# Expert stage of a hybrid decoder layer: a written-out order of blocks, a fifth row buffer and paired keys

## The chip, the core and the metric

The kernel runs on one core of a Trainium2 chip. Its engines are TensorE (PE, with its weight loads as PEld), VectorE (DVE), ScalarE (ACT), GpSimd (POOL) and SyncE (SP); SP issues most transfers, POOL issues the ones that fetch rows by index. The metric is the device time of one execution in microseconds. Before the change the median of three executions is 2899.98 us (2895.31 to 2903.27).

## The reference, cut to what matters

One layer over 1024 tokens of width 1024. A mixing part (projection, pooling, a chunked scan, output projection) is followed by retrieval among 16384 single-neuron experts, and a last norm.

```python
q = (hf @ w_query).reshape(T, 8, 2, 128)
s1, s2 = q[:, :, 0] . sub_keys1, q[:, :, 1] . sub_keys2      # 128 scores each
v1, i1 = top_k(s1, 16); v2, i2 = top_k(s2, 16)
cand = v1[..., :, None] + v2[..., None, :]
top_s, pos = top_k(cand, 16); idx = i1 * 128 + i2 at pos
gates = softmax(top_s)                                       # 8 heads x 16 experts a token
u = expert_down[idx]; act = gelu(hb . u); v = expert_up[idx]
y = sum(gates * act * v);  x = x + gate_f * y;  out = rmsnorm(x, norm_final)
```

## The kernel before, in words

The 1024 tokens are eight tiles of 128. The front (`front`, three groups of tiles) does the mixing part, the query projection and, per head, the two lists of 16 best keys (`top16`); `select` turns the lists of one tile into experts and gates.

The experts are reached in two ways. Tiles 1 to 4 (`DT`) are **dense**: `select` builds one-hot matrices (names `hota`, `hotb`, `hotc`, L826 to L843) and from them a table of gates over all 16384 experts in memory (`gd`), and the loop of `experts` then multiplies the 512 tokens with every expert. One turn of it is a **block** of 128 experts: `raw` (512 KB of down weights) is loaded and split into a high part `dnh` (ACT, L1023) and a low part `dnl` (DVE, L1024); the **first product** is 24 matmuls into `m` (L1033); ACT takes GELU (L1036) and DVE multiplies by the gates (L1037), which gives `w`; the **second product** adds `w` times `up` (512 KB) into eight outputs of 128x512 (L1007, two passes each for one block). Four outputs stay in PSUM (`res`), four are made in two rotating buffers (`rot`) and added by DVE to sums `ys` in SBUF (L1012, L1014). Blocks are grouped in units of three (`SB`), and a unit's whole second product stands behind the first product of the next unit's first block.

Tiles 0, 5, 6 and 7 (`GT`) are **gathered**: for each of a tile's 128 expert slots POOL fetches one row of 8 KB for each token (1 MB in all, L907) into one of four row buffers; DVE takes the dot product with the token (L910), ACT the GELU and the gate (L911, L912), and DVE adds the second half of the row to `yacc` (L903); the buffer is then free. Tile 0 goes first in another form (`ahead`): half rows, first all dots and then all adds (L870, L875, L879), as far as possible during the front. `finish` scales, adds the residual, norms and stores a tile. Tiles 6 and 7 have their `top16` and `select` inside the loop.

The order on each engine is made by a scheduler that runs the program on a timeline of its own, takes what is ready by priority, and so mixes the loop with the steps of the gathers, which `drain` emits at a low priority after each block. Each engine runs its list strictly in order. Pools of the expert stage are laid over memory of the front, and each tile waits until what lay there is done. `rows` turns through the row buffers: three of their own and `row3` (in the pool `more`) once `experts` has begun.

Of the kernel before, what the change touches and what calls it, by code (L numbers as in the profile page):

```python
# [44 lines left out]
LEAD = 2  # L45
# [3 lines left out]
MORE = 1  # L49
# [16 lines left out]
class Trunk:  # L66
    def __init__(self, ctx, tc, I, out):
        self.ctx, self.tc, self.nc, self.I, self.out = ctx, tc, tc.nc, I, out
        self.bg = []
        self.due, self.owed, self.few = 0, 0, 2  # L70
        self.early, self.taken = None, 0

# [30 lines left out]


    def consts(self):
# [9 lines left out]
        self.rooms = {name: self.pool(name) for name in ("rz", "rx", "rp", "r1")}  # L115
# [269 lines left out]
    def front(self, gi):  # L385
# [183 lines left out]
        for b in range(16):  # L569
            if gi + 1 < len(GROUPS):  # L570
                if b == 0:
                    xs = self.loads(gi + 1)
                if b == NB:
                    self.scaled(xs)
                    ahead = self.norm1(gi + 1, xs)
                if b >= NB + 2:
                    next(ahead, None)
            wq = self.wload(I["w_q"][b])
            acc = psa.tile([128, 512], FT, name="acc")
            for k in range(KB):  # L580
# [12 lines left out]
            keys = self.kp.tile([128, 128], FT, name="keys")  # L593
            nc.sync.dma_start(keys, I["keysT"][:, b])
            sp = pss.tile([128, 512], FT, name="ss")
            for i in range(n):
                nc.tensor.matmul(sp[:, i * 128:(i + 1) * 128], q[:, i * 128:(i + 1) * 128], keys,
                                 start=True, stop=True)
            self.drain(rate)
            self.fetch(self.frate)  # L600
            sc = self.sp.tile([128, 3, 128], FT, name="sc")
            nc.scalar.activation(sc[:, :n].rearrange("p a b -> p (a b)"), sp[:, :T], AF.Copy)
            for i in range(n):
                if tiles[i] in LATE:
# [3 lines left out]
                scr = self.tp.tile([128, 128], FT, name="tscr", bufs=2)  # L608
                self.top16(sc[:, i], v[:, b // 2, b % 2], pi[:, b // 2, b % 2], scr)
# [98 lines left out]
    def selects(self, lp):  # L708

        for t, v, pi in self.late:  # L710
            for h in range(0, 8, 2):
                sc = lp.tile([128, 4, 128], FT, name="sc")
                self.nc.sync.dma_start(sc, self.scd[LATE.index(t), :, 2 * h:2 * h + 4])
                for b in range(4):
                    scr = self.tp.tile([128, 128], FT, name="tscr", bufs=2)
                    self.top16(sc[:, b], v[:, h + b // 2, b % 2], pi[:, h + b // 2, b % 2], scr)
                    if b % 2:
                        yield
            yield from self.select(t, v, pi)
# [14 lines left out]
    def select(self, t, v, pi):  # L734
# [15 lines left out]
        key = tp.tile([128, 8, 2, 16], BF, name="key")  # L750
        nc.vector.tensor_copy(key, pi)
# [3 lines left out]
        for h in range(8):  # L755
            scr = tp.tile([128, 128], FT, name="tscr", bufs=2)
            self.top16(cand[:, h], top[:, h], pos[:, h], scr[:, :NCAND])
            if h % 2:
                yield
# [12 lines left out]
        for start, length in ROWS:  # L772
            nc.vector.tensor_scalar(q, p, float(start), float(length - (start == SINGLE)), op0=OP.is_ge, op1=OP.mult)
            nc.vector.tensor_tensor(r2, r2, q, op=OP.subtract)
            if start < SINGLE:
                nc.vector.tensor_scalar(q, p, float(start), None, op0=OP.is_ge)
                nc.vector.tensor_tensor(r1, r1, q, op=OP.add)  # L777
        yield
        idx = tp.tile([128, 2, 8, 16], FT, name="idx")
        for j, r in enumerate((r1, r2)):  # L780
            for h in (0, 4):
# [4 lines left out]
                nc.vector.tensor_tensor(oh, oh, key[:, hs, j].unsqueeze(3).to_broadcast([128, 4, 16, 16]), op=OP.mult)  # L786
# [101 lines left out]
    def gather(self, j):  # L888
# [3 lines left out]
        h2 = gp.tile([128, D], FT, name="h2", bufs=1)  # L892
        nc.sync.dma_start(h2, self.h2r[j * 128:(j + 1) * 128, :])
# [11 lines left out]
        for s in range(128):  # L905
# [9 lines left out]
            prev = (u, a, s)  # L915
            yield
        add(*prev)
# [5 lines left out]
        self.finish(t, [acc[:, :512], acc[:, 512:]], rows, self.residual(xx[:, :D], t), xx[:, D:])  # L923
        yield

    def finish(self, t, y, rows, x, tmp, soon=False):
# [3 lines left out]
        for h in range(2):  # L930
# [3 lines left out]
            self.square(tmp[:, hs], x[:, hs], sums[:, 0, h + 1:h + 2])  # L934
        ss = sums[:, 1, 1:2]
        nc.vector.tensor_reduce(ss, sums[:, :1, :3], axis=AX.X, op=OP.add)  # L936
        rs = self.rsqrt(ss, 1)
        for h in range(2):
# [3 lines left out]
            nc.sync.dma_start(self.out[t * 128:(t + 1) * 128, hs], x[:, hs])  # L942

# [10 lines left out]
    def experts(self):  # L954
# [5 lines left out]
        self.more = self.pool("more", reuse_waits="tile")  # L960
        kinds = {"ys": ([128, 512], FT, len(outs) - 4), "up": ([128, D], FT, SB + 4),
                 "gates": ([128, TD // TC, GS, TC], FT, 2), "h2h": ([128, KB, TD], FR, 1), "h2l": ([128, KB, TD], FR, 1),
                 "raw": ([128, D], FT, 3), "dnh": ([128, D], FR, 2), "dnl": ([128, D], FR, 2),
                 "w": ([128, TD], FT, SB + 1)}
# [4 lines left out]

        rot = self.pool("prot", 2, space=PSUM)  # L970
        res = self.pool("pres", 1, space=PSUM)
        pm1 = self.pool("pm1", 2, space=PSUM)
        held = {o: res.tile([128, 512], FT, name=f"res{i}") for i, o in enumerate(outs[:4])}
# [8 lines left out]
        lp = self.pool("late", 2, reuse_waits="tile")  # L982
        self.bg += [self.early, self.mixed(self.gather(EARLY), self.selects(lp), 3)]
        self.bg += [self.gather(j) for j in range(EARLY + 1, len(GT))]
        steps = 129 * len(GT) - self.taken + 40
        gates = None
        done = 0
        queue = []
# [4 lines left out]
        def mm2(u, ws, some=outs):  # L993
            for o in some:
# [13 lines left out]
                if whole:  # L1008
                    sums[o] = ps
                elif o in ysum:  # L1010
                    if u == 0:
                        nc.vector.tensor_copy(ysum[o], ps)  # L1012
                    else:
                        nc.vector.tensor_tensor(ysum[o], ps, ysum[o], op=OP.add)  # L1014

        b = 0
        for u, size in enumerate(units):
            ws = []
            for j in range(size):
                raw = new("raw")  # L1020
                nc.sync.dma_start(raw, I["downT"][b])
                dn = new("dnh"), new("dnl")
                nc.scalar.activation(dn[0], raw, AF.Copy)  # L1023
                nc.vector.tensor_tensor(dn[1], raw, dn[0].bitcast(FT), op=OP.subtract)  # L1024
                if b % GS == 0:
                    gates = new("gates")
                    nc.sync.dma_start(gates, self.gd[b // GS])
                up = new("up")
                nc.sync.dma_start(up, I["ud"][b * 128:(b + 1) * 128, D:])
                p1 = pm1.tile([128, 512], FT, name="m1")  # L1030
                for n, (x, y) in enumerate(((0, 0), (1, 0), (0, 1))):
                    for k in range(KB):
                        nc.tensor.matmul(p1, dn[x][:, k * 128:(k + 1) * 128], h2[y][:, k],  # L1033
                                         start=(k == 0 and n == 0), stop=(k == KB - 1 and n == 2))
                act = new("w")
                nc.scalar.activation(act, p1, AF.Gelu)  # L1036
                nc.vector.tensor_tensor(act.rearrange("p (c t) -> p c t", t=TC),  # L1037
                                        act.rearrange("p (c t) -> p c t", t=TC), gates[:, :, b % GS], op=OP.mult)
                ws.append((act, up))
                if queue and j == (u == last):  # L1040
                    mm2(*queue.pop())
                b += 1
                want = min(steps * b // (NK - SB * LEAD), steps)
                self.drain(want - done)
                done = want
            queue.append((u, ws))
# [3 lines left out]
        sums = dict(held)  # L1050
        for i in reversed(range(nt)):
            mm2(*queue[0], [(i, 0), (i, 1)])
# [88 lines left out]
```

## Time and profile before

| | |
|---|---|
| median of three executions | 2899.98 us |
| profiled execution, whole | 2912.44 us |
| its span, first to last instruction | 2910.6 us |
| TensorE busy | 2663.1 us (91%) |
| VectorE busy | 2375.6 us (82%) |
| bytes moved | 893.31 MB, mean 307 GB/s |

The profiled execution is 2 us longer than its span and 12 us longer than the median. The front takes about the first 1200 us, the dense loop runs from 1221 us, and what follows its last first product, at 2791 us, is a tail of 120 us. A share of busy time is a mean over these stages, so each is read by itself.

### The profile page before, as it was taken

Reading aid. Unit: us, or ns where it says so; the run is one execution under the profiler, and the core shown is the slowest. Engines: PE = TensorE matmul, PEld = TensorE weight load, DVE = VectorE, ACT = ScalarE, POOL = GpSimd, SP = SyncE. Lnnn points to the kernel's source line nnn. Section 1 sums busy time; section 2 is a strip of 40 time slices with the busy share of each in tenths; the row PEclk is TensorE's granted clock in tenths of the full one; section 3 lists DMA queues with packets and bytes.
Section 4 is the critical chain, followed back from the end, with each engine's and each line's share of the span. In section 5 each row is a group of like instructions: output and inputs, shape, how many; then the busy total and the mean of one; then the engine's idle time right before and its main releaser. Section 6 shows DMA issues by size and latency. Waiting matters only on the chain. (4 is left out here: it accounts for less than half of the span.)

```text
span 2910.6 us, 31644 instructions
## 1 busy us (share of the span) xinstructions
PE 2663.1 (91%) x10243; PEld 1746.7 (60%) x10244; DVE 2375.6 (82%) x5156; ACT 830.1 (29%) x2244; POOL 884.6 (30%) x679
## 2 busy tenths in 40 slices
PE   8899986789889989699999999999999999999961
PEld 5688555676557876465655666666666666666630
DVE  6625898979999879899999777787877777778887
ACT  3523451322254342322222222222222222222211
POOL 0000066554440005022333333333333333333343
PEclk9999987899989989899999999999999999999985
DMA  8655389999863679888999999899999989998986
GB/s 304 222 172 173 103 296 331 356 362 361 289 234 124 185 220 383 277 310 323 352 354 356 356 366 337 336 364 361 346 348 351 370 320 372 348 368 339 356 320 234
DMA packets 264278, 893.31 MB, mean 307 GB/s; under 512 B 25904, under 2 KB 110000, under 8 KB 212656
## 3 DMA queue, kind: packets, MB, share of 16 engines
q0 software_dynamic: 92448, 541.11, 49.0%
q1 hardware_dynamic: 171664, 350.18, 34.7%
q8 instruction: 81, 1.33, 0.2%
q14 instruction: 85, 0.70, 0.1%
HBM read 840.86 MB, written 50.34 MB: 306 GB/s over the span
## 5 line engine op out<-in xcount | busy, mean ns | idle before, releaser
L907 POOL DMA_INDIRECT row<-in_ud,eidx x384 | 547.5, 1426 | 1105.8 <-DVE yacc L903 870.4
L903 DVE SCALAR_TENSOR_TENSOR yacc<-row,act,yacc 128x1024 f32<-128x1024 f32 x381 | 488.5, 1282 | 67.9 <-ACT act L912 65.1
L910 DVE SCALAR_TENSOR_TENSOR row<-row,h 128x1024 f32<-128x1024 f32 x384 | 467.1, 1218 | 51.1 <-DMA row<-in_ud,eidx 50.8
L1007 PE MATMUL rot<-up,w 128*128 128x512 f32 x1024 | 464.5, 596 | 4.8 <-DVE ys L1014 4.8
L1007 PE MATMUL res<-up,w 128*128 128x512 f32 x1024 | 458.6, 592 | 0.0
L870 POOL DMA_INDIRECT row<-in_ud,eidx x256 | 313.6, 1225 | 417.3 <-DVE rkb L777 102.1
L911 ACT ACTIVATE act<-act 128x1 f32<-128x1 f32 x384 | 77.1, 201 | 976.0 <-DVE row L910 975.6
L1007 PEld LDWEIGHTS rot<-up,w 128*128 128x128 f32 x1024 | 194.9, 191 | 221.8 <-issue 208.3
L1007 PEld LDWEIGHTS res<-up,w 128*128 128x128 f32 x1024 | 193.8, 189 | 200.5 <-issue 189.4
L1033 PE MATMUL m<-h2h,dnh 128*128 128x512 f32 x1024 | 292.9, 427 | 18.9 <-ACT dnh L1023 18.9
L1033 PE MATMUL m<-h2l,dnh 128*128 128x512 f32 x1024 | 285.6, 413 | 0.0
L1033 PE MATMUL m<-h2h,dnl 128*128 128x512 f32 x1024 | 279.6, 412 | 0.0
L1033 PEld LDWEIGHTS m<-h2h,dnh 128*128 128x128 f32 x1024 | 193.5, 189 | 96.8 <-issue 39.5
L307 PE MATMUL acc<-wraw,r 128*128 128x256 f32 x1024 | 239.3, 388 | 8.3 <-ACT s L525 8.3
L435 PE MATMUL acc<-r,wraw 128*128 128x384 f32 (+1 forms) x768 | 235.0, 464 | 2.3 <-ACT s L439 1.3
L581 PE MATMUL acc<-rz,wraw 128*128 128x384 f32 (+1 forms) x768 | 235.3, 457 | 0.0
L1033 PEld LDWEIGHTS m<-h2l,dnh 128*128 128x128 f32 x1024 | 192.6, 188 | 66.5 <-issue 30.4
L1033 PEld LDWEIGHTS m<-h2h,dnl 128*128 128x128 f32 x1024 | 193.4, 189 | 59.2 <-issue 19.1
L307 PEld LDWEIGHTS acc<-wraw,r 128*128 128x128 f32 x1024 | 196.3, 195 | 37.9 <-ACT s L525 9.9
L1014 DVE TENSOR_TENSOR ys<-rot,ys 128x512 f32<-128x512 f32 x168 | 115.4, 687 | 112.1 <-PE rot L1007 111.6
L435 PEld LDWEIGHTS acc<-r,wraw 128*128 128x128 f32 x768 | 147.7, 195 | 81.8 <-issue 8.6
L581 PEld LDWEIGHTS acc<-rz,wraw 128*128 128x128 f32 x768 | 143.7, 194 | 64.0 <-issue 2.3
(298 smaller groups left out, 3271.3 us busy)
## 6 DMA issues: line engine op xcount, KB each, us to landing
up<-in_ud SPq DMA_DIRECT2D x128, 512.0 KB, 7.4
raw<-in_downT SPq DMA_DIRECT2D x128, 512.0 KB, 7.9
gd<-stage SPq DMA_DIRECT2D x32, 1024.0 KB, 9.3
gates<-gd SPq DMA_DIRECT2D x16, 2048.0 KB, 12.3
wraw<-in_w_c SPq DMA_DIRECT2D x48, 512.0 KB, 5.6
wraw<-in_w_q SPq DMA_DIRECT2D x48, 512.0 KB, 6.3
wraw<-in_w_o SPq DMA_DIRECT2D x36, 512.0 KB, 5.2
row<-in_w_ada SPq DMA_DIRECT2D x32, 512.0 KB, 5.3
```

Of the source, the lines that this page charges most:

```text
L307: self.nc.tensor.matmul(acc[i], a(4 * kp + j, slice(i * 128, (i + 1) * 128)), ws[:, j * 256:(j + 1) * 256], start=kp == kps[0] and j == 0 ...
L435: nc.tensor.matmul(acc[:, :T], wc[:, k * 128:(k + 1) * 128], h[:, k], start=k == 0, stop=k == KB - 1)
L581: nc.tensor.matmul(acc[:, :T], wq[:, k * 128:(k + 1) * 128], g[:, k], start=k == 0, stop=k == KB - 1)
L870: nc.gpsimd.indirect_dma_start(out=u[:, i * D:(i + 1) * D], out_offset=None, in_=src, in_offset=bass.IndirectOffsetOnAxis(ap=e[:, s + i:s ...
L903: nc.vector.scalar_tensor_tensor(acc, u[:, D:], a, acc, op0=OP.mult, op1=OP.add)
L907: nc.gpsimd.indirect_dma_start(out=u, out_offset=None, in_=self.I["ud"], in_offset=bass.IndirectOffsetOnAxis(ap=e[:, s:s + 1], axis=0))
L910: nc.vector.scalar_tensor_tensor(u[:, :D], u[:, :D], 1.0, h2, op0=OP.mult, op1=OP.mult, accum_out=a)
L911: nc.scalar.activation(a, a, AF.Gelu)
L1007: nc.tensor.matmul(ps, w[:, ts], up[:, hs], start=st, stop=sp, skip_group_check=True)
L1014: nc.vector.tensor_tensor(ysum[o], ps, ysum[o], op=OP.add)
L1033: nc.tensor.matmul(p1, dn[x][:, k * 128:(k + 1) * 128], h2[y][:, k], start=(k == 0 and n == 0), stop=(k == KB - 1 and n == 2))
```

## The change

1. Order. From the first block on, every PE, DVE and ACT instruction of the loop is tied to the one before it (`in_order`): the three engines keep the program's order there. SP and POOL are still ordered by the scheduler.
2. The loop is written as a pipeline: raw weights are loaded three blocks ahead, the high part is made two ahead, the low part one ahead, the gates are multiplied one block late, and the second product of a unit is cut in thirds (3, 3 and 2 outputs) behind the first products of the next unit; DVE's additions of `rot` come one block later.
3. Gathers. Tile 0 is drained wholly ahead of the loop. The 384 gather steps of tiles 5, 6, 7 are spread evenly over blocks 4 to 125 (`FIRST`, `LAST`), at most five in a block; one step of `selects` goes to eight of a gather (`MIX`), for the tile that comes next. A gathered tile is finished on DVE, in two steps.
4. A fifth row buffer (`MORE = 2`); the two of the pool `more` are now laid behind the loop's other pools, which themselves stand in another order.
5. `select`: keys are kept twice, side by side, so that the product of one-hot and key reads pairs; a compare and an add become one instruction; one scratch buffer `tscr` for two.

```diff
-LEAD = 2
+FIRST, LAST = 4, 2
+MIX = 8
-MORE = 1
+MORE = 2
...
-        self.rooms = {name: self.pool(name) for name in ("rz", "rx", "rp", "r1")}
+        self.rooms = {name: self.pool(name) for name in ("rx", "rp", "r1", "rz")}
...
-                nc.vector.tensor_scalar(q, p, float(start), None, op0=OP.is_ge)
-                nc.vector.tensor_tensor(r1, r1, q, op=OP.add)
+                nc.vector.scalar_tensor_tensor(r1, p, float(start), r1, op0=OP.is_ge, op1=OP.add)
...
-                nc.vector.tensor_tensor(oh, oh, key[:, hs, j].unsqueeze(3).to_broadcast([128, 4, 16, 16]), op=OP.mult)
+                pairs = oh.rearrange("p h r (a b) -> p (h r) a b", b=2)
+                nc.vector.tensor_tensor(pairs, pairs, key[:, j, hs].rearrange("p h r d -> p (h r) d").unsqueeze(2)
+                                        .to_broadcast([128, 64, 8, 2]), op=OP.mult)
...
-        self.bg += [self.early, self.mixed(self.gather(EARLY), self.selects(lp), 3)]
-        self.bg += [self.gather(j) for j in range(EARLY + 1, len(GT))]
+        self.bg.append(self.early)
+        self.drain()
+
+        start = len(nc.cur_bb.bb.instructions)
+        for j in range(EARLY, len(GT)):
+            late = [s for s in self.late if j + 1 < len(GT) and s[0] == GT[j + 1]]
+            self.bg.append(self.mixed(self.gather(j), self.selects(lp, late), MIX))
+        total = 128 * (len(GT) - EARLY)
...
+                want = total * max(b + 1 - FIRST, 0) // (NK - LAST - FIRST) - self.count
+                want = max(min(want, 5), 0)
+                load(b + 3)
...
+                gated(b - 1)
+                if b % GS == 1:
+                    gload(b // GS + 1)
+                steps(min(want, 1))
+                added()
+                if todo:
+                    n = -(-len(todo) // (size - j))
+                    mm2(u - 1, queue, todo[:n])
+                    todo = todo[n:]
+                    if n > 3:
+                        added()
+                steps(min(max(want - 1, 0), 1))
+                low(b + 1)
+                steps(max(want - 2, 0))
+                acts[b] = new("w")
+                nc.scalar.activation(acts[b], p1, AF.Gelu)
+                high(b + 2)
...
+        gated(NK - 1)
+        added()
+        self.in_order(start)
```

What this does to the order is seen at three places. First POOL, at the end of the front, where `h2h` and `h2l` are the tokens of the dense tiles, `sums` are small cells of the norm, and rows from `in_ud` by `eidx_66` are tile 0's half rows. Before:

```order
L978 DMA h2l<-h2td 128x4096
L870 DMA row_9619<-in_ud,eidx_66 128x1024 x2
L870 DMA row_9707<-in_ud,eidx_66 128x1024 x2
...
L870 DMA row_9912<-in_ud,eidx_66 128x1024 x2
L870 DMA row_9955<-in_ud,eidx_66 128x1024 x2
L933 TENSOR_TENSOR row_9963<-row_9963 128x512 x2
L340 MEMSET sums 128x4 x4
```

And of the change, at the same place:

```order
L1016 DMA h2l<-h2td 128x4096
L353 MEMSET sums 128x4 x3
L892 DMA row_9418<-in_ud,eidx_66 128x1024
L892 DMA row_9423<-in_ud,eidx_66 128x1024 x2
L892 DMA row_9418<-in_ud,eidx_66 128x1024
L892 DMA row_9443<-in_ud,eidx_66 128x1024 x2
...
L892 DMA row_9508<-in_ud,eidx_66 128x1024 x2
L935 DMA row_9749<-in_ud,eidx 128x2048
L935 DMA row_9767<-in_ud,eidx 128x2048
```

The last 32 half rows of tile 0 stood ahead of the cells of `sums`, and stand behind them now (16 rows of two, of which `...` leaves out 13), with tile 5's first gathers right behind.

Second DVE at the same time. Before, tile 0's last additions lie between the one-hots of the front, a hundred rows ahead of the loop's first row:

```order
L879 SCALAR_TENSOR_TENSOR yacc<-row_9912,acts,yacc 128x1024
L828 TENSOR_TENSOR hotc<-hotb,etr 128x1024
L829 TENSOR_TENSOR hotb<-hotb,etr 128x1024
L879 SCALAR_TENSOR_TENSOR yacc<-row_9955,acts,yacc 128x1024 x2
L826 TENSOR_TENSOR hota<-keyno,etr 128x1024
L827 TENSOR_TENSOR hotb<-keyno,etr 128x1024
L932 TENSOR_TENSOR row_9963<-yacc,row_9960 128x512 x2
```

Of the change, in the loop's blocks 2 to 4 (`w` is the product with the gates, L1061 frees a `rot`, `dnl` at the end belongs to block 5):

```order
L1061 COPY ys<-rot 128x512
L1085 TENSOR_TENSOR dnl<-raw,dnh 128x1024
L901 SCALAR_TENSOR_TENSOR yacc<-row_9423,acts,yacc 128x1024
L901 SCALAR_TENSOR_TENSOR yacc<-row_9428,acts,yacc 128x1024 x2
L1090 TENSOR_TENSOR w<-w,gates 128x512
L901 SCALAR_TENSOR_TENSOR yacc<-row_9433,acts,yacc 128x1024 x2
...
L901 SCALAR_TENSOR_TENSOR yacc<-row_9508,acts,yacc 128x1024 x2
L968 TENSOR_TENSOR row_9516<-yacc,row_9513 128x512 x2
L938 SCALAR_TENSOR_TENSOR row_9749,act<-row_9749,h_9746 128x1024
L1061 COPY ys<-rot 128x512
```

38 additions of tile 0 have moved from the front into the loop; 32 of them stand between block 3's product with the gates and the copy that frees a `rot` for block 4, with only tile 0's finish and tile 5's first dot between.

Third DVE where one gathered tile follows another; of the change:

```order
L931 SCALAR_TENSOR_TENSOR yacc<-row_12770,act,yacc 128x1024
L1090 TENSOR_TENSOR w<-w,gates 128x512
L968 TENSOR_TENSOR row_12796<-yacc,row_12793 128x512
L969 TENSOR_TENSOR row_12796<-row_12796 128x512
...
L977 SCALAR_TENSOR_TENSOR row_12796<-row_12796,rs_y,row_12793 128x512 x2
L1063 TENSOR_TENSOR ys<-rot,ys 128x512
L816 SCALAR_TENSOR_TENSOR eidx<-idx 128x128
L938 SCALAR_TENSOR_TENSOR row_12867,act<-row_12867,h_12791 128x1024
L1085 TENSOR_TENSOR dnl<-raw,dnh 128x1024
```

The next tile's indices (`eidx`) are made one instruction ahead of its first dot, and a low part `dnl` stands behind that dot.

## Rows read from the trace of the kernel before

**Rows 1.** the page: span, engines, the queue of gathers, loads to landing
```profile
span 2910.6 us, 31644 instructions
...
q0 software_dynamic: 92448, 541.11, 49.0%
...
up<-in_ud SPq DMA_DIRECT2D x128, 512.0 KB, 7.4
...
gates<-gd SPq DMA_DIRECT2D x16, 2048.0 KB, 12.3
```

**Rows 2.** stretches: length, busy of engines (instructions), PE clock, DMA share, GB/s
```profile
1100.00:1160.00 60.00, 60.00 (x302) 39.17 (x301) 57.89 (x113) 14.64 (x29) 30.17 (x23) 1.00 1.05 392
...
1200.00:1240.00 40.00, 19.63 (x75) 14.42 (x76) 35.57 (x165) 10.61 (x15) 0.28 (x4) 0.70 0.96 344
1300.00:1600.00 300.00, 295.22 (x945) 178.20 (x944) 286.69 (x668) 73.24 (x191) 98.88 (x69) 0.99 0.92 347
1600.00:2000.00 400.00, 400.00 (x1293) 243.48 (x1292) 308.00 (x395) 93.39 (x250) 137.06 (x95) 1.00 0.92 352
...
2804.00:2880.00 76.00, 6.54 (x16) 2.60 (x14) 57.40 (x71) 11.93 (x48) 33.64 (x22) 0.57 0.89 333
```

**Rows 3.** TensorE in order of time, 2795 to 2911: start, length, [idle before]
```profile
2807.80 2.74 PE L1007 MATMUL rot<-up,w 128*128 128x512 f32 x6
2881.54 2.07 PE L1002 MATMUL rot<-ys,ident 128*128 128x512 f32 x2 [71.00 <-DVE dnl L932]
...
2888.24 2.74 PE L1007 MATMUL rot<-up,w 128*128 128x512 f32 x6
```

**Rows 4.** groups of the loop, 1240 to 2790: busy, mean ns | idle before
```profile
L903 DVE SCALAR_TENSOR_TENSOR yacc<-row,act,yacc 128x1024 f32<-128x1024 f32 x352 | 450.6, 1280 | 59.9 <-ACT act L912 57.9 <-DVE yacc L903 0.5
...
L910 DVE SCALAR_TENSOR_TENSOR row<-row,h 128x1024 f32<-128x1024 f32 x356 | 433.1, 1218 | 40.3 <-DMA row<-in_ud,eidx 40.0
...
L1024 DVE TENSOR_TENSOR dnl<-raw,dnh 128x1024 fp32r<-128x1024 f32 x125 | 153.7, 1229 | 10.6 <-ACT dnh L1023 9.2
...
L786 DVE TENSOR_TENSOR oh<-oh,key 128x1024 bf16<-128x1024 bf16 x8 | 9.7, 1218 | 0.1
...
L784 DVE TENSOR_TENSOR oh<-ranks,rkc 128x1024 bf16<-128x1024 bf16 x4 | 2.8, 688 | 0.1
```

**Rows 5.** waits of VectorE, 1600 to 2790: total us, times, longest us
```profile
DVE yacc L903 <- ACT act L912: 55.6, 93, 0.6
...
DVE row L910 <- DMA row<-in_ud,eidx: 27.6, 17, 3.8
```

**Rows 6.** gathers of 1600 to 2790, from issue to landing
```profile
DMA to landing us min/median/max: 2.6/8.5/15.6
```

**Rows 7.** GpSimd in order of time at the front's end
```profile
1150.78 1.26 POOL L870 DMA_INDIRECT row<-in_ud,eidx  x1 [0.30 <-issue]
1205.22 0.17 POOL L340 MEMSET sums<- 128x4 f32 x3 [27.42 <-DVE top L704]
...
1247.03 0.96 POOL L907 DMA_INDIRECT row<-in_ud,eidx  x1 [39.36 <-DVE v L704]
```

**Rows 8.** SyncE at the same time: last gate table stored, first gates loaded
```profile
1205.81 0.62 SPq L848 DMA_DIRECT2D gd<-stage  x1
...
1217.92 0.33 SPq L1027 DMA_DIRECT2D gates<-gd  x1
```

**Rows 9.** tile 0's half rows, issued on GpSimd, 1090 to 1161
```profile
L870 POOL DMA_INDIRECT row<-in_ud,eidx x29 | 38.4, 1324 | 24.4 <-DVE yacc L879 10.7 <-issue 5.5 <-DVE tscr L703 5.3
```

**Rows 10.** tile 0's additions on VectorE, 1100 to 1172
```profile
L879 DVE SCALAR_TENSOR_TENSOR yacc<-row,acts,yacc 128x1024 f32<-128x1024 f32 x30 | 38.2, 1273 | 0.2
```

**Rows 11.** first products alone (L1033), 1220 to 1303
```profile
1220.00:1303.00 83.00, 50.22 (x192) 38.02 (x192) 0.96 0.85 322
```

**Rows 12.** second products alone (L1007), 1220 to 1303
```profile
1220.00:1303.00 83.00, 35.94 (x82) 15.73 (x83) 0.96 0.85 322
```

**Rows 13.** second products alone (L1007), 2000 to 2400
```profile
2000.00:2400.00 400.00, 232.48 (x522) 98.84 (x522) 1.00 0.91 350
```

More of the change, by code (lines that the diff above doesn't have):

```diff
@@ L102, in fetch, with in_order @@
             self.taken += 1
+    def in_order(self, start):
+        last = {}
+        order = mybir.DependencyInfo(mybir.DependencyClass.NoSync, mybir.DependencyReason.DATA)
+        for ins in list(self.nc.cur_bb.bb.instructions)[start:]:
+            if ins.engine in (mybir.EngineType.PE, mybir.EngineType.DVE, mybir.EngineType.Activation):
+                if ins.engine in last:
+                    self.tc.add_manual_dep(ins, last[ins.engine], order, reason="order")
+                last[ins.engine] = ins.name
     def consts(self):
@@ L922, in gather, with finish, finishing @@
         xx = self.row()
[L923 removed]
+        x = self.residual(xx[:, :D], t)
+        add(*prev)
         yield
[L926 removed]
+        yield from self.finishing(t, [acc[:, :512], acc[:, 512:]], rows, x, xx[:, D:], True)
+    def finish(self, *args):
+        for _ in self.finishing(*args):
+            pass
+    def finishing(self, t, y, rows, x, tmp, soon=False):
         nc = self.nc
@@ L991, in experts, with mm2 @@
         last = len(units) - 1
-        def mm2(u, ws, some=outs):
+        order = [o for pair in zip(outs[4:], outs[:4]) for o in pair]
+        sums = dict(held)
+        adds = []
+        def mm2(u, ws, some):
             for o in some:
@@ L1010, in mm2, with added, load, gload @@
                 elif o in ysum:
[L1011 to L1014, printed above, removed]
+                    adds.append((u, o, ps))
+        def added():
+            while adds:
+                u, o, ps = adds.pop(0)
+                if u == 0:
+                    nc.vector.tensor_copy(ysum[o], ps)
+                else:
+                    nc.vector.tensor_tensor(ysum[o], ps, ysum[o], op=OP.add)
+        raws, highs, lows, ups, acts, gates = {}, {}, {}, {}, {}, {}
+        def load(b):
+            if b < NK:
+                raws[b] = new("raw")
+                nc.sync.dma_start(raws[b], I["downT"][b])
+        def gload(g):
+            if g < NK // GS:
+                gates[g] = new("gates")
+                nc.sync.dma_start(gates[g], self.gd[g])
+        def high(b):
+            if b < NK:
+                highs[b] = new("dnh")
+                nc.scalar.activation(highs[b], raws[b], AF.Copy)
+        def low(b):
+            if b < NK:
+                lows[b] = new("dnl")
+                nc.vector.tensor_tensor(lows[b], raws.pop(b), highs[b].bitcast(FT), op=OP.subtract)
+        def gated(b):
+            if b >= 0:
+                w = acts[b].rearrange("p (c t) -> p c t", t=TC)
+                nc.vector.tensor_tensor(w, w, gates[b // GS][:, :, b % GS], op=OP.mult)
+        def steps(n):
+            end = self.count + n
+            for _ in range(n + 1):
+                if self.count < end:
+                    self.drain(1)
+        for b in range(3):
+            load(b)
+        gload(0)
+        high(0)
+        high(1)
+        low(0)
+        queue = None
         b = 0
@@ L1018, in experts @@
             ws = []
+            todo = list(order) if queue else []
             for j in range(size):
[L1020 to L1027, printed above, removed]
```

94 lines of the change are left out of this document (47 added, 47 removed).

## The prediction, made before the change was run

> **What bounds the kernel now.** I read the stretches first, because a mean over the span mixes three stages. In the loop TensorE is the bound: 400.00 of 400 us busy at a granted clock of 1.00, beside 308 us of VectorE and a DMA share of 0.92 [rows 2]. At both ends it is not. In 1200 to 1240 TensorE works 19.63 of 40 us at a mean clock of 0.70 while VectorE works 35.57; behind 2804 it works 6.54 of 76 us while VectorE works 57.40 and the DMA engines are 0.89 busy [rows 2]. Then TensorE in order of time: after the passes at 2807.80 it stands for 71.00 us until 2881.54, and the releaser is VectorE's L932, a step of a tile's `finish` [rows 3]. So the loop's last additions of `rot` stand in VectorE's list behind the last gathered tile, and the 71 us are gathers that the loop did not take along. Why not? In 1600 to 2000 POOL issued 95 instructions, nearly all gathers [rows 2], one in 4.2 us. VectorE waited for a landing row only 27.6 us in 1190, 17 times [rows 5], with 8.5 us from issue to landing in the middle [rows 6]. Transfers therefore do not set that pace; VectorE's order and the four buffers do. Buffers are free again only when the add is through.
>
> A block lasts 12.26 us: 522 passes in 400 us [rows 13] are 32.6 blocks of 16 passes. A pass takes 0.445 us (232.48 / 522), and a first product 5.1 us ((400 - 232.48) / 32.6).
>
> **The tail, -81 us.** If all gathers end inside the loop, TensorE goes on at 2807.80 + 2.74 = 2810.5 [rows 3]; the last 16 passes at 0.457 (2.74 / 6) take 7.3, to 2817.9. Behind the last six passes of before there were still 2910.6 - 2890.98 = 19.6 us [rows 1, 3], in which VectorE also had the gathered tile behind it; I take 12 for a dense tile's finish alone, 2829.9, that is -81. Bounds: -71, if only the stall goes, and -85.
>
> **The start, +39 us.** This is where the order moves work the wrong way. Before, tile 0's last half rows were issued during the front (one at 1150.78; 29 in 1090 to 1161 at 1.324 us each [rows 7, 9]) and VectorE did its additions there (30 at 1.273 us [rows 10]). Now 32 half rows stand on POOL behind the cells of `sums`, which before started only at 1205.22, after 27.42 us of waiting for the front's `top16` (L704) [rows 7]; and 38 additions stand in the loop's blocks 2 to 4, 32 of them ahead of the copy that frees a `rot` for block 4. That copy, hence TensorE, waits for all this.
> VectorE's clock: the last gate table is stored at 1205.81, the first `gates` are loaded from 1217.92 [rows 8] and land about 12.3 later [rows 1], 1230. The product with the gates waits for that, and the additions stand behind it. Then 12 to 20 us of other rows (low parts at 1.229 [rows 4], products and copies), 38 x 1.273 = 48.4, tile 0's finish on VectorE, about 6 by ten rows of half that size, and the first dot, 1.2 [rows 4]: 1298 to 1306, middle 1302. POOL's clock: from 1205, 32 x (1.324 + the 0.30 between two issues [rows 7]) = 52, to 1257, then the first gather's landing at 8.5 [rows 6]: earlier than VectorE, so VectorE sets it, with 1288 to 1315 as bounds (gates 10 us earlier, or all later).
> What is lost by 1303? Before had done 192 matmuls of first products, that is 8 blocks, and 82 passes [rows 11, 12]. After can have done five first products and 28 passes (16 of the first unit, 12 of the next before both `rot` are full). 3 x 5.1 + 54 x 0.445 = 39 us. Bounds +26 to +52, by the stall's end.
>
> **The front, -10.** The product of one-hot and key (L786) takes 1218 ns today; the compare that already reads in the paired shape of the same 1024 bf16 elements takes 688 [rows 4]. Four a tile (8 for the two tiles of the loop) save 2.1 us a tile, about 10 for the five tiles of the front. The saved adds of ranks are small. The additions moved out relieve VectorE by another 38 us [rows 10], but in 1100 to 1160 TensorE was itself busy for 60.00 of 60 [rows 2], so I count none of it. Bounds: -25 and +5 (`tscr`, now one buffer for two, serialises).
>
> **Where one gathered tile follows another, +16.** `eidx` is made one row ahead of the next tile's first dot, so no gather of that tile can be under way. VectorE stands for an issue (0.96 [rows 7]) and a landing (8.5, up to 15.6 [rows 6]) right after a finish of 6 and the one-hots of about 5, and `dnl` of the next block is queued behind: 21 us against one block of lead, 12.3. TensorE then has nothing in the high parts' stead: 8 us, twice. Below: nothing, if indices and gathers go earlier than the row on VectorE suggests. Above: 25 in all.
>
> **The pace, +5.** 384 gathers over 122 blocks are 3.15 a block, one in 3.90 us. VectorE: 308 / 32.6 = 9.45 us a block with 95 / 32.6 = 2.91 gathers; 0.24 more at 1.280 + 1.218 [rows 4] give 10.05. The selects of two tiles, for 84 blocks, add about 1.2, the waits for ACT's gate 0.6 each [rows 5] about 0.5: 11.8 of 12.26. That holds, narrowly. An in-order engine at 96% is late now and then; 5 us, bounds 0 and 25. Buffers: a row is held for issue 0.96, landing 8.5, dot, gate and add 3, and the rows of VectorE's list between, some 3: 15.5. Five buffers turn in 19.5, four in 15.6. The fifth hides the landing; without it each late landing would reach VectorE.
> Thirds of the second product, loads three blocks ahead and high parts two ahead remove no work from TensorE; where it is full already they are worth nothing, and their cover is TensorE's own 12.26 us a block. The steps on ACT have room (93 of 400 us [rows 2]).
>
> **DMA.** A block needs 0.524 MB each of `raw` and `up`, 0.262 of `gates` (a load of 2048 KB for eight blocks [rows 1]) and 3.15 x 1.049 of rows: 4.61 MB, 376 GB/s over 12.26 us. The loop moved 352, but 392 was sustained over the 60 us of 1100 to 1160 [rows 2]; I take this row, because there the queues were loaded, and count nothing.
>
> **Sum.** -81 + 39 - 10 + 16 + 5 = -31: span 2880, whole profiled execution 2912.4 - 31 = 2881. The runs' median lies 12.5 us below the profiled execution today, so 2869.
>
> **Rivals.**
> *The other side: transfers.* If rows at five in flight do not come faster than before's 352 GB/s, a block takes 4.61 / 0.352 = 13.1 us, 0.84 more; 122 blocks are +102 in place of the +5, and the time is 2966. It decides from 0.30 us a block (36 / 122), that is below 367 GB/s. For it: a share of 0.92 in all of the loop [rows 2], and 0.89 in the tail with nothing but gathers in the way. Against: 392 GB/s [rows 2], and VectorE hardly waiting for rows [rows 5]. By the Trainium skill, "DMA: Bandwidth & Descriptors", section "Where 436 GB/s comes from", transfers between HBM and SBUF are bound by the HBM side at about 358 GB/s; the trace disagrees with 392 over 60 us [rows 2], though no row has it for longer. As a mechanism here, that limit would make a block 12.9 us, an estimate from that page, and the time about 2939. The chance of this rival is 0.13.
> *VectorE becomes the bound* while selects are mixed in (the first 84 blocks): at 12.26 + 0.3 us a block, or stalls at each boundary and at each unit's `rot`, 25 to 40 us more, 2891 to 2909: no change that can be told. For it: 286.69 of 300 us busy in 1300 to 1600, with selects [rows 2]. Chance 0.11.
> *The start costs nothing*: the additions fit where VectorE waits for gates and for the front, or the front ends by their 38 us earlier [rows 10]. Then -31 - 39, 2830. For it: VectorE busy 57.89 of 60 in 1100 to 1160 [rows 2]. Against: POOL's cells wait for `top16`, whose end is the front's. Chance 0.12.
>
> **How the numbers follow.** The forecast has 0.64, by itself 2846 to 2891 (the bounds of start and boundaries, added as independent ones). About 0.3%, 9 us, is what a measurement of this kernel can tell from no change. Faster: 0.64 + 0.12 = 0.76; same 0.11; slower 0.13. The range 2832 to 2906 leaves out the transfers' rival and half of the free start.
>
> **What the profile after would show.** Behind the last first product about 40 us instead of 120, without a wait of 71. A gap on TensorE ending near 1303, released by the copy that frees `rot`, with L901 ahead of it on VectorE. Two gaps of about 8 us near blocks 45 and 86. Gathers 3.9 us apart, 370 GB/s or more. The product with the keys at about 690 ns. VectorE over 90% busy in the first 84 blocks. I am wrong if TensorE has idle time in every block (transfers or VectorE), if the first gathers run before 1240, or if VectorE still has gathers behind the last block.

## The result, and the profile after

The median of six executions is 2883.62 us (2882.19 to 2888.18), beside 2899.16 us for the kernel before: a ratio of 0.9942, 95% interval 0.9925 to 0.9958. That is 15.5 us faster; 2869 was forecast, and the measured time lies inside the stated range of 2832 to 2906. The profiled execution of the changed kernel took 2882.19 us, 1.4 us less than its median. Its page begins:

```profile
span 2880.4 us, 31445 instructions
```

The forecast for this span was 2880. So the sum came out on the trace (in part by luck, as the section on the prediction shows), and the step from the trace to the median did not; the first experiment below is on that. First the stretches, with the columns of [rows 2]:

```profile
1200.00:1240.00 40.00, 27.35 (x94) 18.40 (x95) 32.01 (x54) 3.09 (x4) 10.72 (x9) 0.81 0.73 254
1240.00:1300.00 60.00, 15.24 (x43) 8.30 (x41) 47.07 (x54) 4.36 (x13) 31.88 (x29) 0.67 0.93 360
1300.00:1600.00 300.00, 298.28 (x957) 181.63 (x958) 269.98 (x467) 73.09 (x202) 94.67 (x77) 0.99 0.96 376
1600.00:2000.00 400.00, 388.49 (x1246) 235.94 (x1245) 355.66 (x615) 99.37 (x269) 123.78 (x100) 0.99 0.93 367
...
2804.00:2880.00 76.00, 58.48 (x165) 31.23 (x163) 47.68 (x103) 13.72 (x38) 8.10 (x8) 0.92 0.32 118
```

The hole has moved. Behind 2804 TensorE works 58.48 of 76 us where it worked 6.54 [rows 2]; in 1240 to 1300 it works 15.24 of 60, where before it was full:

```profile
1240.00:1300.00 60.00, 60.00 (x207) 38.80 (x206) 57.91 (x192) 13.94 (x34) 13.12 (x13) 1.00 0.83 310
```

In 1300 to 1600 the kernel now moves 376 GB/s (347 before), in 1600 to 2000 VectorE is busy 355.66 of 400 us (308), and TensorE is no longer full there: 388.49. TensorE's waits from 1200 on, in all, times, longest:

```profile
PE rot L1051 <- DVE ys L1061: 37.8, 1, 37.8
PE rot L1051 <- issue: 23.7, 1, 23.7
PE rot L1051 <- DVE ys L1063: 16.2, 5, 8.7
PE m L1120 <- DVE dnl L1085: 8.6, 1, 8.6
```

Where the 71.00 us of [rows 3] stood at the end, 37.8 and 23.7 stand at the start and 8.6 at a tile boundary. The 23.7, for which the profile names no releaser, end at 1212.65, just behind VectorE's first product with the gates; a wait at the start is not new, as the kernel before has one of 18.9 there:

```profile
PE m L1033 <- ACT dnh L1023: 18.9, 1, 18.9
```

TensorE in order of time at the start:

```profile
1240.01 2.74 PE L1051 MATMUL res<-up,w 128*128 128x512 f32 x6
1280.54 4.45 PE L1051 MATMUL rot<-up,w 128*128 128x512 f32 x6 [37.80 <-DVE ys L1061]
...
1301.72 5.49 PE L1051 MATMUL rot<-up,w 128*128 128x512 f32 x6 [8.69 <-DVE ys L1063]
```

What that copy (L1061) waited for is on POOL, the cells of `sums`, tile 0's last half rows (L892) and tile 5's first gather (L935):

```profile
1182.38 0.17 POOL L353 MEMSET sums<- 128x4 f32 x3 [146.14 <-DMA up<-in_ud]
...
1224.69 1.35 POOL L892 DMA_INDIRECT row<-in_ud,eidx  x1 [30.66 <-DVE eidx L816]
...
1263.96 1.02 POOL L892 DMA_INDIRECT row<-in_ud,eidx  x1 [0.30 <-DMA row<-in_ud,eidx]
1269.71 1.86 POOL L935 DMA_INDIRECT row<-in_ud,eidx  x1 [4.74 <-DVE yacc L901]
```

The memset had held POOL for 146 us (before, 29 half rows were issued within that time [rows 9]), and the last half row goes out at 1263.96, where before it was 1150.78 [rows 7]. Four half rows go out from 1189.21 on; then POOL waits 30.66 us for VectorE, whose first additions in the loop (from 1220.76) stand behind the product with the gates. VectorE meanwhile: the first product with the gates, the 32 additions, tile 5's first dot and a later one:

```profile
1211.85 0.69 DVE L1090 TENSOR_TENSOR w<-w,gates 128x512 f32<-128x512 f32 x1 [7.36 <-DMA gates<-gd]
...
1232.50 42.23 DVE L901 SCALAR_TENSOR_TENSOR yacc<-row,acts,yacc 128x1024 f32<-128x1024 f32 x32
...
1278.32 1.55 DVE L938 SCALAR_TENSOR_TENSOR row<-row,h 128x1024 f32<-128x1024 f32 x1 [2.26 <-DMA row<-in_ud,eidx]
...
1298.63 1.23 DVE L938 SCALAR_TENSOR_TENSOR row<-row,h 128x1024 f32<-128x1024 f32 x1 [8.90 <-DMA row<-in_ud,eidx]
```

The copy for `rot` follows the first of these dots, the additions for `rot` that end the wait of 8.7 follow the second. SyncE, the last gate table and the first gates:

```profile
1189.97 0.38 SPq L870 DMA_DIRECT2D gd<-stage  x1
1204.05 0.79 SPq L1075 DMA_DIRECT2D gates<-gd  x2
```

They stand 16 and 14 us earlier than in [rows 8]. Now VectorE and then TensorE where tile 6 follows tile 5:

```profile
1802.14 0.28 DVE L816 SCALAR_TENSOR_TENSOR eidx<-idx 128x128 int32<-128x128 f32 x1
1812.40 1.22 DVE L938 SCALAR_TENSOR_TENSOR row<-row,h 128x1024 f32<-128x1024 f32 x1 [9.98 <-DMA row<-in_ud,eidx]
...
1813.55 1.22 DVE L1085 TENSOR_TENSOR dnl<-raw,dnh 128x1024 fp32r<-128x1024 f32 x1
```
```profile
1804.29 1.98 PE L1120 MATMUL m<-h2l,dnh 128*128 128x512 f32 x8
1814.83 3.78 PE L1120 MATMUL m<-h2h,dnl 128*128 128x512 f32 x8 [8.55 <-DVE dnl L1085]
```

This is the order's third place in time: indices, a dot that waits 9.98 us for its row, a low part queued behind it, and TensorE waiting for that. Last, VectorE's wait for rows in 1600 to 2790, for [rows 5], and the product with the keys in 1240 to 2790, for [rows 4]:

```profile
DVE row L938 <- DMA row<-in_ud,eidx: 50.7, 31, 10.0
```
```profile
L807 DVE TENSOR_TENSOR oh<-oh,key 128x1024 bf16<-128x1024 bf16 x8 | 5.5, 691 | 0.3
```

### The profile page after: what moved, and what is told of

The parts are those of the page before. It is cut to its first block, busy times and chain, and to the rows that moved or that the text cites. A ratio compares the mean times of both kernels' runs of the same rounds, so it can differ in the third digit from the quotient of the medians.

```text
span 2880.4 us, 31445 instructions
## 1 busy us (share of the span) xinstructions
PE 2648.1 (92%) x10244; PEld 1728.6 (60%) x10244; DVE 2365.3 (82%) x5106; ACT 832.7 (29%) x2247; POOL 804.2 (28%) x673
## 4 chain that ended last, share of the span: by engine, by line
PE 61%; DVE 13%; issue 11%; DMA 7%; POOL 6%; ACT 1%; SPq 0%; POOLq 0%; DVEq 0%; ACTq 0%
PE m L1120 17%; PE rot L1051 12%; PE res L1051 11%; PE acc L320 7%; PE acc L594 5%; DMA row<-in_ud,eidx 4%; PE acc L448 4%; POOL row L892 3%; POOL row L935 3%; DVE yacc L901 2%; DVE row L897 1%; PE g L865 1%; DMA gd<-stage 1%; DVE yacc L931 1%; DVE s L483 1%
## 5 line engine op out<-in xcount | busy, mean ns | idle before, releaser
L935 POOL DMA_INDIRECT row<-in_ud,eidx x384 | 480.8, 1252 | 1018.8 <-DVE yacc L931 965.1
L1051 PE MATMUL rot<-up,w 128*128 128x512 f32 x1024 | 477.5, 601 | 79.2 <-DVE ys L1061 37.8
L1051 PE MATMUL res<-up,w 128*128 128x512 f32 x1024 | 470.1, 594 | 1.4 <-DVE w L1090 1.4
L892 POOL DMA_INDIRECT row<-in_ud,eidx x256 | 310.9, 1214 | 355.8 <-PE tr L666 99.2
L1120 PE MATMUL m<-h2h,dnh 128*128 128x512 f32 x1024 | 309.3, 444 | 0.5 <-ACT dnh L1080 0.5
L1120 PE MATMUL m<-h2h,dnl 128*128 128x512 f32 x1024 | 255.5, 392 | 8.7 <-DVE dnl L1085 8.7
L1120 PE MATMUL m<-h2l,dnh 128*128 128x512 f32 x1024 | 253.6, 390 | 0.0
```

What stands on the lines that cost most here:

```text
L892: nc.gpsimd.indirect_dma_start(out=u[:, i * D:(i + 1) * D], out_offset=None, in_=src, in_offset=bass.IndirectOffsetOnAxis(ap=e[:, s + i:s ...
L935: nc.gpsimd.indirect_dma_start(out=u, out_offset=None, in_=self.I["ud"], in_offset=bass.IndirectOffsetOnAxis(ap=e[:, s:s + 1], axis=0))
L1051: nc.tensor.matmul(ps, w[:, ts], up[:, hs], start=st, stop=sp, skip_group_check=True)
L1120: nc.tensor.matmul(p1, x[b][:, k * 128:(k + 1) * 128], h2[y][:, k], start=(k == 0 and n == 0), stop=(k == KB - 1 and n == 2))
```

## Experiments

To place a gain or a loss I compare TensorE's work done by a given time: first products at 5.1 us for 24 matmuls and second-product passes at 0.445 us, the prices worked out in the prediction. A ratio is to the kernel before in the same set of runs; that kernel's median moved from 2898.3 to 2901.8 us between sets, so a difference in us between two experiments is good to some 3 us.

**The kernel before, profiled once more** (no edit).

> The kernel before, unchanged: a second profiled execution. The prediction took 12.5 us off the profiled execution's time to reach the median of the runs, for the changed kernel too. Theory A: those 12.5 us belong to that one execution (a slow draw), so this execution lies near the median, span 2893 to 2904, and a row of the first trace shows where the surplus was, most likely in the last gathers (the wait of 71 us behind 2810) or in the front. Theory B: a profiled execution of this kernel is always about 12 us longer than an unprofiled one: span near 2910 again.

Its span is 2898.5, the execution 2900.29. Theory A holds: the 12 us belong to the first profiled execution (one more execution shows it, and the changed kernel's own, 1.4 us below its median, agrees). TensorE's longest wait and the first gates:

```profile
PE rot L1002 <- DVE dnl L932: 72.5, 1, 72.5
```
```profile
1209.65 0.33 SPq L1027 DMA_DIRECT2D gates<-gd  x1
```

The tail is as long as before (72.5 for 71.00); the surplus lay at the start, the second of the two places guessed: the gates are loaded 8.3 us earlier than in [rows 8], and 5.6 us, not 14, behind the changed kernel's. First products and then passes in the first trace of before, in this one, in the changed kernel's, and in an experiment further down without the tie (e10); stretch, length, busy time and count of matmuls and of weight loads, clock, DMA:

```profile
1160.00:1600.00 440.00, 200.02 (x757) 144.55 (x758) 0.97 0.89 327
...
1160.00:1600.00 440.00, 204.00 (x454) 86.07 (x454) 0.97 0.89 327
```
```profile
1160.00:1600.00 440.00, 202.16 (x768) 146.27 (x768) 0.97 0.90 336
1600.00:2770.00 1170.00, 606.90 (x2280) 428.92 (x2280) 1.00 0.92 351
...
1160.00:1600.00 440.00, 213.49 (x481) 90.77 (x482) 0.97 0.90 336
1600.00:2770.00 1170.00, 672.66 (x1512) 286.38 (x1511) 1.00 0.92 351
```
```profile
1160.00:1600.00 440.00, 181.16 (x720) 135.05 (x720) 0.92 0.92 351
1600.00:2770.00 1170.00, 564.85 (x2232) 420.38 (x2232) 0.99 0.94 372
...
1160.00:1600.00 440.00, 191.74 (x421) 82.06 (x422) 0.92 0.92 351
1600.00:2770.00 1170.00, 657.59 (x1490) 282.83 (x1489) 0.99 0.94 372
```
```profile
1160.00:1600.00 440.00, 211.82 (x840) 157.45 (x840) 0.99 0.88 329
...
1160.00:1600.00 440.00, 224.29 (x499) 96.32 (x500) 0.99 0.88 329
```

By 1600, from 1160 on, the kernel before has done 768 / 24 x 5.1 + 481 x 0.445 = 377.2 us of work here (in the first trace 362.9), the changed kernel 720 / 24 x 5.1 + 421 x 0.445 = 340.3: the start costs 36.9 us. From 1600 to 2770 it is 1157.3 against 1137.4: the loop costs 19.9. It ends 18.1 earlier, so the end gives back 36.9 + 19.9 + 18.1 = 74.9.

**Tile 0's rows back in the front** (e2).

```diff
-        self.rows += range(ROWBUFS, ROWBUFS + MORE)
...
         self.bg.append(self.early)
         self.drain()
+        self.rows += range(ROWBUFS, ROWBUFS + MORE)
```

> The changed kernel, but the two row buffers over the front's memory join the three others only when tile 0's rows have been emitted; then the program's order again has all of tile 0's half rows on GpSimd ahead of the cells of sums, and its additions on VectorE in the front. Theory A (the start costs what waits for tile 0's last rows): TensorE's waits of 37.8 and 8.7 us near block 4 go, the front's end comes back by part of the 38 additions (up to 16 us later), net about 15 to 23 us less than the changed kernel: 2861 to 2869. Rival: VectorE bounds the front's end, so that the 48 us of additions there delay the gate tables by as much as the wait was: 2880 to 2890, no change.

2871.64 us, 0.9892 (0.987 to 0.9913) of before, 12 us less than the changed kernel. The wait of 37.8 is gone, but the gain lies below theory A's interval, and the reason is the rival's. SyncE:

```profile
1242.55 0.81 SPq L1075 DMA_DIRECT2D gates<-gd  x2
```

With the additions ahead of the last one-hots, the first gates are loaded 38.5 us later than in the changed kernel. All additions now run by 943 us, on a VectorE that is busy 99.91 of 100 us from 800 to 900, and the one-hots come later by that. In the kernel before the same additions stand between the one-hots, and its gates come at 1209.65: what counts is where in VectorE's list they stand. Both theories were half right.

**Indices earlier** (e3), and **both edits** (e4).

```diff
-MIX = 8
+MIX = 7
```

> The changed kernel, but one step of the selects to seven of a gather, not eight: the indices of the next gathered tile are ready some ten gathers before that tile's first dot. Theory A (at the two tile boundaries TensorE waits because VectorE stands for the first row of the next tile): the excess of the blocks at both boundaries, 15 and 6 us by the trace, goes: 2863 to 2869. Rival: the boundary is lost to the finish and its rows on VectorE, not to the landing, and the selects squeezed into fewer blocks make VectorE late elsewhere: 2880 to 2890.

2865.22 us, 0.9871 (0.9851 to 0.9892): 18.4 us less than the changed kernel. TensorE's wait for `dnl` falls from 8.6 to 0.2. Theory A.

> Both edits together (tile 0's rows in the front, and one select step to seven gathers). Theory A: the two gains are of different stretches and add: 2842 to 2855. Rival: one gives back the other (a loop that starts earlier meets the same front end, or VectorE is full in the first 84 blocks), so that no more than the larger single gain shows: 2861 or more.

2858.54 us, 0.9855 (0.9836 to 0.9873): 25 us, between the two theories. The 5 us that are missing to 12 + 18 = 30 are no more than the intervals leave open, but the trace has a place for them: at the second boundary, where a block lasts 18.35 us for a usual 13.2, VectorE now waits for something else, the residual of the finish:

```profile
2288.86 0.69 DVE L969 TENSOR_TENSOR row<-row 128x512 f32<-128x512 f32 x1 [11.42 <-DMA row<-x1d]
```

**Four row buffers** (e5).

```diff
-MORE = 2
+MORE = 1
```

> The changed kernel with four row buffers in place of five. Theory A (a row is held for about 15.5 us: issue, landing 8.5, dot, gate, add and rows of VectorE between; at 3.9 us a gather four buffers turn in 15.6): VectorE waits for rows often, more than the 71 us in 41 waits of the changed kernel, and passes lateness to TensorE: 10 to 40 us more, 2894 to 2924. Rival: transfers follow so closely that four buffers do (before had four and waited for rows only 27.6 us): 2880 to 2890, and the fifth buffer is worth nothing.

2942.15 us, 1.0152 (1.0127 to 1.0178): 58.5 us more than the changed kernel, theory A and beyond its range. VectorE's wait for rows, in the changed kernel 71.0 us in 41 times over the whole loop:

```profile
DVE row L938 <- DMA row<-in_ud,eidx: 232.7, 154, 9.0
```

Without the fifth buffer the whole change is a loss.

**The old keys and ranks in the changed kernel** (e6), and **the new ones in the kernel before** (e7).

```diff
-                pairs = oh.rearrange("p h r (a b) -> p (h r) a b", b=2)
-                nc.vector.tensor_tensor(pairs, pairs, key[:, j, hs].rearrange("p h r d -> p (h r) d").unsqueeze(2)
-                                        .to_broadcast([128, 64, 8, 2]), op=OP.mult)
+                nc.vector.tensor_tensor(oh, oh, key[:, hs, j].unsqueeze(3).to_broadcast([128, 4, 16, 16]), op=OP.mult)
```

> The changed kernel with the old product of one-hot and key and the old two-instruction rank. Theory A (VectorE bounds the end of the front, and the five selects there each save 2.1 us by the pairs and some by the ranks): 5 to 15 us more, 2889 to 2899, the first gates loaded that much later. Rival: the front's end is bound by TensorE and by transfers, the selects are hidden: 2880 to 2887.

> The kernel before with only the paired product and the one-instruction rank. Theory A: VectorE bounds the front there too and sets the tail by the last gathers: the front's 10 us and 4 us of the two selects of the loop come off, 2884 to 2893 against 2900. Rival: the scheduler orders the front anew and the saved time goes into other waits: 2896 to 2904.

e6: 2907.23 us, 1.0031 (1.002 to 1.0042), 23.6 us more than the changed kernel. e7: 2899.43 us, 1.0 (0.9988 to 1.0013), no gain. So the same edit is worth nothing in the kernel before and more than the net gain in the changed one. The first gates of e6 and of e7:

```profile
1214.68 0.81 SPq L1074 DMA_DIRECT2D gates<-gd  x2
```
```profile
1212.92 0.33 SPq L1028 DMA_DIRECT2D gates<-gd  x1
```

In e6 they come 10.6 us later than in the changed kernel, theory A's front; that is one trace against one, and the kernel before's two differ by 8.3. In e7 they are no earlier than in the second trace of before (1209.65): there the rival holds. By work done (692 matmuls of first products and 400 passes by 1600, 2213 and 1486 from there to 2770), 15.3 of the 21.2 us between the spans of e6 and of the changed kernel are lost by 1600 and 5.8 in the loop: besides the gates a longer start (the wait for the copy that frees `rot` is 40.8) and a longer second boundary (the block there lasts 23.9 us, 18.7 in the changed kernel).

**The pace of before** (e9): 20 steps left behind the last block.

```diff
-FIRST, LAST = 4, 2
+FIRST, LAST = 4, -7
```

> The changed kernel, its 384 gather steps spread at 2.93 a block, before's pace, in place of 3.15, so that some 20 steps are left behind the last block. Theory A (the tail is what the gathers left over take): 20 gathers at 3 to 3.5 us and the last finish stand between the last block and the end, 50 to 70 us more than the changed kernel: 2934 to 2954. Rival: before's tail was not the number of gathers left, but VectorE's order (the last additions of rot behind a whole tile), which the tied order takes away by itself: 2880 to 2905.

2919.06 us, 1.0073 (1.0046 to 1.01): 35 us more, between the two. TensorE behind the last block:

```profile
2887.11 2.08 PE L1046 MATMUL rot<-ys,ident 128*128 128x512 f32 x2 [51.74 <-DVE dnl L968]
```

The tail is back: from the last first product to the end 96.1 us (2915.2 - 2819.1) against 37.1 (2880.4 - 2843.3), 59 more, as theory A has it. But the last first product ends 24 us earlier. About 12 of them are gained behind the copy for `rot`, in block 5, which lasts 13.61 us and 25.11 in the changed kernel; about 9 at the tile boundaries, which cost 11 us together and 20 there. Theory A left out that with fewer gathers a block such disturbances cost less.

**Without the tie** (e10).

```diff
-        self.in_order(start)
```

> The changed kernel without the tie of the three engines to the program's order: the same program, ordered by the scheduler. Theory A (the tie keeps the additions of rot, the low parts and the products with the gates out from behind gathers): the scheduler's own order puts gathers late or early again, TensorE waits in the loop or at its end, 15 to 50 us more than the changed kernel: 2898 to 2934. Rival: the even spread of the steps over the blocks does it, and the scheduler keeps that by itself: 2876 to 2890.

2936.49 us, 1.0118 (1.0095 to 1.0142): 53 us more, theory A and just beyond its range. The rows above show what I did not expect: by 1600 this order has done 840 / 24 x 5.1 + 499 x 0.445 = 400.6 us of work, 60 more than the changed kernel, and from 1600 to 2770 (2232 matmuls, 1534 passes) another 19.5. All of it and 54 more are lost at the end:

```profile
2906.49 2.07 PE L1046 MATMUL rot<-ys,ident 128*128 128x512 f32 x2 [134.42 <-DVE dnl L968]
```

The scheduler again puts gathers last: one is issued at 2893.9, and the last first product ended at 2753.2. The tie is what keeps them in the loop, and what makes the start wait.

**The extra buffers' pool first, with the earlier indices** (e11).

```diff
+        self.more = self.pool("more", reuse_waits="tile")
         pools = {kind: self.pool("d_" + kind, bufs, reuse_waits="tile") for kind, (_, _, bufs) in kinds.items()}
...
-        self.more = self.pool("more", reuse_waits="tile")
```

> The changed kernel with one select step to seven gathers, and with the pool of the two extra row buffers ahead of the loop's other pools again, as before: they lie over memory of the front that is free earlier, so 18 of the 38 additions come back to the front, spread between its last one-hots, and 20 stay in the loop. Theory A (the start is a sum of the front's end on VectorE and of the additions behind it; spread additions fill VectorE's idle time): better than all of them in the front ahead of the one-hots (2858.5): 2840 to 2856. Rival: VectorE has the same work to do until the first dot wherever the additions stand: 2857 to 2867.

2848.22 us, 0.9808 (0.9784 to 0.9832): the best kernel here, 35 us below the changed one and 17 below e3, theory A. By 1600 it has done 748 / 24 x 5.1 + 448 x 0.445 = 358.3 us of work, 18 more than the changed kernel. Its start is still not free, since with the moved pools the tokens `h2l` are loaded at 1208.6 (at 1035.7 in the changed kernel):

```profile
PE m L1120 <- DMA h2l<-h2td: 31.8, 1, 31.8
```

**Gathers pressed into 110 blocks** (e8, both edits as the base).

```diff
-FIRST, LAST = 4, 2
+FIRST, LAST = 4, 14
```

> The version with both edits (tile 0's rows in the front, one select step to seven gathers), its gathers pressed into 110 blocks, 3.49 a block: 4.97 MB a block, 402 GB/s at 12.36 us. Theory A (VectorE is the next bound): 9.45 + 0.58 x 2.5 + 1.3 for selects and 0.5 of waits are 12.7 us a block in the first 75 blocks, and TensorE loses 20 to 40 us by waits for VectorE: 2878 to 2898 against 2858.5. Rival 1 (transfers are the next bound, at 390 or below): the same loss, but VectorE waits for rows most of the time. Rival 2: both have room: 2855 to 2864.

2902.83 us, 0.9999 (0.9986 to 1.0012): 44 us more than its base. VectorE's wait for rows, and one stretch:

```profile
DVE row L938 <- DMA row<-in_ud,eidx: 90.8, 77, 8.1
```
```profile
2400.00:2650.00 250.00, 250.00 (x811) 152.55 (x810) 225.63 (x288) 66.16 (x187) 92.74 (x73) 1.00 1.01 410
```

In 2400 to 2650, with no selects, 410 GB/s are moved and TensorE is full. Rival 1 puts the ceiling at 390, so it falls. The loss lies where selects are mixed in: from 1600 to 2400 TensorE waits for VectorE 39.5 us, in the base 10.2. VectorE's own wait for rows rises there from 43.4 to 53.2, so late rows can be some 10 of these 29 us; for the rest VectorE is the next bound, at a higher price than worked out.

**The tie from block 6 on** (e12, on e11).

```diff
-        start = len(nc.cur_bb.bb.instructions)
...
+                if b == 6:
+                    start = len(nc.cur_bb.bb.instructions)
```

> The version with the two extra buffers' pool first and one select step to seven gathers, with one more edit: the three engines are tied to the program's order only from block 6 on, and the scheduler orders the blocks before. Theory A (without the tie the first blocks are not held up by tile 0's additions, as the untied run showed with 60 us more of TensorE's work done by 1600; here 31.8 us of its start are a wait for h2l that stays, and some 15 to 20 us of waits for w and ys can go): 2830 to 2844 against 2848. Rival: VectorE's additions only move behind the first blocks and make TensorE wait at blocks 6 to 8 instead: 2844 to 2854.

2851.89 us, 0.9831 (0.9814 to 0.9847): nothing gained against e11, the rival. The wait for `h2l` stays, and the rest moves:

```profile
PE m L1121 <- DMA h2l<-h2td: 31.5, 1, 31.5
PE m L1121 <- DVE dnl L1084: 12.9, 1, 12.9
```

## Why the prediction was right, and where it was off

Direction and mechanism held, and the gain is half of what was forecast. By its steps, against the second trace of before, which lies at the median:

- *The tail, -81*: measured -74.9 by work done (-73 against the first trace). The wait of 71 us is gone; 37.1 us behind the last first product where about 40 were forecast. e9 and e10 show that gathers left over are what the tail was.
- *The start +39, the front -10*: together +29 forecast, +36.9 measured (+22.6 against the first trace, whose own start was late). Place and chain are as described: cells of `sums` (held, by the profile, by a load of `up` and not by `top16`), half rows, additions, the copy that frees `rot`. The times were not: the half rows began at 1189, not 1205, and the waits ended at 1280.5 and 1301.7, not in one at 1303. The second wait is a term that the prediction had at nothing: it let tile 5's first rows land under the additions, but the first was issued only at 1269.71, when an addition had freed a buffer, and VectorE waited 2.26 us for it and 8.90 for a later one. e2 shows that the additions cannot simply be put back ahead of the one-hots, since the front then ends 38.5 us later.
- *The boundaries, +16*: the loop's loss of 19.9 is all there. The block at the first boundary lasts 26.15 us (first products from 1802.03 to 1828.18), 13 more than the usual 13.2 of a block with three outputs, the one at the second 18.65, 5.4 more, where 8 and 8 were forecast; e3 takes 18.4 off by earlier indices alone.
- *The pace, +5*: nothing is left for it beside the boundaries. VectorE is busy 269.98 of 300 and 355.66 of 400 us, 90 and 89%, where "over 90%" was forecast. The fifth buffer was rightly called necessary, and given no price: it is worth 58.5 us by e5.
- *DMA, nothing*: right. 376 and 367 GB/s were moved where 347 and 352 were before, and 410 in e8. The Trainium skill's "DMA: Bandwidth & Descriptors", section "Where 436 GB/s comes from", names about 358 GB/s, half of a stack's 716, as what binds transfers between HBM and SBUF. The traces disagree, with 376 over 300 us here and 410 over 250 in e8; no run here shows what the core that has the other half did.
- *From the trace to the median*: this step failed. "The runs' median lies 12.5 us below the profiled execution today, so 2869" carried a property of one execution over to another kernel. A second trace of before has it at 2900.29, and the changed kernel's profiled execution is 1.4 us below its own median. The sum -31 was made against a start 14.3 us worse than usual (362.9 us of work by 1600 against 377.2). With the usual start the terms are -74.9, +36.9 and +19.9, -18.1, beside -15.5 by the medians. That the span came out at 2880 was in part luck: against the first trace, on which the sum was made, the tail gave back 8 us less than forecast and the start and the front cost 6.4 less, and the two misses cancel.

Of the rivals, "transfers" is excluded by 376 GB/s and by e8; "VectorE becomes the bound" did not happen at 3.15 gathers a block, but e8 has most of it at 3.49; "the start costs nothing" is excluded by the wait of 37.8 us and by the 36.9 us of work that are missing by 1600 (22.6 against the first trace).

Open: why the paired keys and shorter ranks give nothing in the kernel before, and why without them the changed kernel loses more than the 10.6 us of its front. The paired product without the shorter ranks, the thirds of the second product and a finish on POOL were not tried by themselves.

## What to carry to other kernels

A fixed order moves a wait rather than removes it: look for what the last block of the old order waited for, and for what now stands ahead of the first block of the new one, and price both. Where a loop leaves an engine near 90% busy, the price of a disturbance depends on that slack: the tile boundaries cost 20 us at 3.15 gathers a block and 11 at 2.93 (e9). The same edit can be worth nothing in one order and more than the whole gain in another (e7, e6), so it is tried in the order in which it will run; why it was so here is not shown. And a sum made against one profiled execution is compared with medians only after a second execution has shown which parts of the first were its own.

## What the runs showed of the hardware

This kernel's one core moved 410 GB/s over 250 us at a DMA share of 1.01 (e8), in gathers of 8 KB rows and loads of 512 and 2048 KB. The start of one and the same program varies between executions: 1217.9 and 1209.7 us for the same load of gates in the kernel before, while the wait in its tail varied by 1.5 us (71.0 and 72.5).
